# A hybrid decoder layer on one core: the matmul order of the attention written out, its steps turned round, projections in small portions

## The chip, the core and the metric

One core of a Trainium2 chip runs the whole program. Its engines are TensorE (PE in the rows; PEld is its weight load), VectorE (DVE), ScalarE (ACT), GpSimd (POOL) and SyncE (SP), which issues most of the DMAs. The metric is the device time of one execution in microseconds (us); less is better.

## The reference

The program computes one decoder layer over 1024 tokens of width 1024 in float32: a mixer with two groups of heads side by side (a chunked state-space scan, "SSD", and a stick-breaking attention of 8 heads of 64), cross attention to 256 memory tokens, and an MLP with squared ReLU. The change is in the stick-breaking attention:

```python
def stick_breaking_attention(q, k, v):
    for i in range(s_len // Q_BLOCK):              # blocks of 128 queries
        ...
        logits = jnp.einsum("bhqd,bhkd->bhqk", qb, kb) * scale
        mask = s_pos < t_pos
        log_stay = jnp.where(mask, jax.nn.log_sigmoid(-logits), 0.0)
        log_beta = jax.nn.log_sigmoid(logits)
        later = lax.cumsum(log_stay, axis=3, reverse=True) - log_stay
        w = jnp.where(mask, jnp.exp(log_beta + later), 0.0)
        outs.append(jnp.einsum("bhqk,bhkd->bhqd", w, vb))
```

A query's weight on an earlier key is the sigmoid of their score times the product of one minus the sigmoids of all keys between them. So a row of weights comes from a running product along the keys.

## The kernel before, in words

**Precision.** Every float32 product is three matmuls: each operand is split into a rounded high half (ScalarE, `act`, L107) and the remainder (VectorE, `tt`, L110), and `mm3` (L208 to L210) multiplies high by high, high by low and low by high. Weights come from memory in pieces of 128 x 512 (`piece`), land in a staging tile `wst`, and are split into `whi` and `wlo`, a ring of six.

**Attention.** Heads are taken one after the other, each in four steps m = 0 to 3. A step has two blocks of 128 queries, i = 2m and 2m + 1, with rows of 128(i + 1) keys, 128 to 1024 wide.
- `stays` makes a step's rows: score matmuls into tiles `z` (two PSUM banks, tag aux), a sigmoid on ScalarE into the row `stay`, and one scan on VectorE (L752) that turns the row into running products. Rows up to 512 wide have two buffers (tag stayS), wider ones two others (stayL).
- `turned` transposes 256 keys of both blocks on TensorE into a tile `wT` (L768; two banks, tag tr), and splits it into `wTh` and `wTl`. The last 256 keys of a step, where the causal edge lies, go into `wlast`, a pair whose unused quarter is set once; the rest is split as one slice of 256 and one of 128 columns.
- `summed` multiplies the turned weights with differences of the values, `vt` and `vl`, into a tile `ops` (L792; one bank, tag m1, OB = 1), four matmuls of 256 columns a block. Two steps share a bank; when both are done ScalarE and VectorE bring it to `oT`.

While a step is turned and summed, the next step's rows are made: `behind` holds the step to be turned, `due` the block to be summed. Per head `load_qk` and `load_v` issue DMAs from GpSimd's queue, and `differ_v` makes the value differences on VectorE and ScalarE.

**Work dealt in.** The projections of later heads and of the memory (`proj_qk`, `proj_v`, `mem_kv`; tiles `qkps`, `vps`, `mkv`, three PSUM banks, tag m0) are generators. `interleave` runs them beside the attention: whichever side has done the smaller share of its total goes on, and `("need", n)` makes the attention wait in the text until n units of projections are written. The units count 8 for each of the four that are left when the attention starts (32), the heads 7; head 7 runs beside the first half of the output projection (`out_first`, tiles `o1`). A projection yields after 24 matmuls, the attention after a whole step.

**What sets the order.** The text only gives priorities. A scheduler, with its own estimate of each instruction's time, takes on every engine the ready instruction of the highest priority; `later` shifts priorities (weight pieces come early, EARLY; splits of turned blocks a little early, WP; evacuations, EV). So single projection matmuls stand wherever the scheduler expected TensorE to wait. The built order is then fixed: each engine runs its instructions in that order.

**After head 7.** The attention's buffers are given back, and there the scaled operands `yB` of the output projection's second half are made from `oT` (four for each half of the tokens, ScalarE and VectorE). The squares of `oT` are summed into `osum`; after the first tiles (`o2`) 8 small matmuls `sps` (L975) sum them over partitions, GpSimd makes the factor `ro` (L226), and VectorE adds the tiles to `h` with it.

## Time and profile before

| | |
|---|---|
| runs | 1345.69, 1348.46, 1349.19 us; median 1348.46 |
| profiled execution | 1352.11 us, of which the span is 1350.4 |
| TensorE / VectorE / ScalarE / GpSimd busy | 1302.1 / 947.5 / 701.2 / 201.2 us |
| attention, first scan to the last widest one | 251.9 to 486.3 us of the span |
| MLP, from there on | 704 to 1341 us |

Times in the rows are from the span's start. An engine's busy time in a stretch is the union of its instructions; for TensorE each matmul's end is modelled and reaches into the next, so its busy time is more than its work. "idle before" tells for how long an engine did nothing ahead of such instructions, and the name behind the arrow ended that wait.

### The profile page before, as it was taken

How to read it: one execution, taken by the hardware profiler on the slowest of the kernel's cores; microseconds unless marked ns; L12 is line 12 of the kernel's file. 1: busy time of each engine (PE TensorE's matmuls, PEld its weight loads, DVE VectorE, ACT ScalarE, POOL GpSimd, SP SyncE). 2: the span in 40 equal slices, each digit the busy share in tenths (PEclk: the TensorE clock that was granted, in tenths of full speed). 3: DMA queues.
4: the chain of work that ended last, by engine and by line, in shares of the span. 5: the costliest groups of instructions: out<-in, count | busy, mean ns of one | idle time of the engine just before them, and what ended most of it. 6: DMA issues, size and time to landing. Idle time of an engine off the chain costs nothing.

```text
span 1350.4 us, 18360 instructions
## 1 busy us (share of the span) xinstructions
PE 1302.1 (96%) x6469; PEld 1067.1 (79%) x6469; DVE 947.5 (70%) x1527; ACT 701.2 (52%) x1341; POOL 201.2 (15%) x228
## 2 busy tenths in 40 slices
PE   8999999989998999999998999999999999999997
PEld 6989887778776788887876888888887787888885
DVE  7758866587689965646579765666667866589785
ACT  7454643465557642566445545544553595444453
POOL 0000000310211011022343323322330000000000
PEclk9999999999999999999999999999999999999999
DMA  6121345852556534121034545345459843633351
GB/s 220 33 71 48 98 124 137 238 161 68 160 149 197 155 101 125 39 56 32 33 140 148 172 156 170 123 145 164 141 172 327 304 131 95 235 95 96 96 156 70
DMA packets 95852, 181.68 MB, mean 135 GB/s; under 512 B 9808, under 2 KB 14992, under 8 KB 95760
## 3 DMA queue, kind: packets, MB, share of 16 engines
q1 hardware_dynamic: 85040, 155.78, 36.2%
q0 software_dynamic: 8624, 18.88, 5.0%
q10 hardware_dynamic: 2096, 5.84, 1.3%
q8 instruction: 51, 0.84, 0.2%
q14 instruction: 41, 0.34, 0.1%
HBM read 128.00 MB, written 52.46 MB: 134 GB/s over the span
## 4 chain that ended last, share of the span: by engine, by line
PE 81%; DVE 8%; ACT 4%; DMA 3%; issue 3%; POOL 1%; SPq 0%; POOLq 0%; ACTq 0%; DVEq 0%
PE P L210 7%; PE P L208 7%; PE P L209 7%; PE pr L208 7%; PE pr L209 7%; PE pr L210 7%; DVE stay L752 2%; PE o L210 2%; PE o L208 2%; PE o L209 2%; PE qkps L208 2%; PE qkps L209 2%; PE qkps L210 2%; DMA wst<-in_wp 2%; PE ops L792 2%
## 5 line engine op out<-in xcount | busy, mean ns | idle before, releaser
L208 PE MATMUL pr<-whi 128*128 128x512 f32 x448 | 175.9, 396 | 3.4 <-ACT whi L107 3.4
L209 PE MATMUL pr<-wlo,whi 128*128 128x512 f32 x448 | 176.9, 395 | 0.1
L210 PE MATMUL pr<-whi,wlo 128*128 128x512 f32 x448 | 176.1, 393 | 0.0
L110 POOL TENSOR_TENSOR c<-c 128x512 f32<-128x512 f32 x60 | 86.6, 1455 | 201.4 <-ACT c L107 199.1
L110 DVE TENSOR_TENSOR wlo<-w1r,whi 128x512 fp32r<-128x512 f32 x92 | 80.2, 874 | 41.9 <-ACT whi L107 41.9
L107 ACT ACTIVATE whi<-w1r 128x512 fp32r<-128x512 f32 x92 | 57.8, 630 | 94.3 <-DVE w1r L110 47.3
L208 PEld LDWEIGHTS pr<-whi 128*128 128x128 f32 x448 | 83.9, 188 | 24.8 <-ACT whi L107 4.3
L210 PE MATMUL P<-T,wlo 128*128 128x512 f32 x256 | 100.9, 394 | 1.2 <-DVE wlo L110 1.2
L208 PE MATMUL P<-T,whi 128*128 128x512 f32 x256 | 100.8, 394 | 0.0
L209 PE MATMUL P<-T,whi 128*128 128x512 f32 x256 | 100.7, 394 | 0.0
L209 PEld LDWEIGHTS pr<-wlo,whi 128*128 128x128 f32 x448 | 84.2, 188 | 20.3 <-DVE wlo L110 1.1
L210 PEld LDWEIGHTS pr<-whi,wlo 128*128 128x128 f32 x448 | 84.1, 188 | 20.2
L107 ACT ACTIVATE whi<-wst 128x512 fp32r<-128x512 f32 (+1 forms) x88 | 54.6, 630 | 78.4 <-PE o L210 30.7
L107 ACT ACTIVATE c<-c 128x512 f32<-128x512 f32 x132 | 81.5, 628 | 25.8 <-DVE c L110 24.2
L752 DVE TENSOR_TENSOR_SCAN stay<-stay,dg 128x128 f32<-128x128 f32 (+3 forms) x64 | 85.3, 1346 | 3.7 <-ACT stay L107 3.3
L107 ACT ACTIVATE whi<-us 128x512 fp32r<-128x512 f32 x64 | 40.3, 630 | 79.7 <-PE pr L209 66.8
L110 DVE TENSOR_TENSOR wlo<-wst,whi 128x512 fp32r<-128x512 f32 (+1 forms) x88 | 61.8, 715 | 24.2 <-ACT whi L107 23.1
L209 PE MATMUL P<-B,whi 128*128 128x512 f32 x192 | 76.5, 398 | 0.0
L208 PE MATMUL P<-B,whi 128*128 128x512 f32 x192 | 76.3, 397 | 0.0
L210 PE MATMUL P<-B,wlo 128*128 128x512 f32 x192 | 76.1, 396 | 0.0
L110 DVE TENSOR_TENSOR wlo<-us,whi 128x512 fp32r<-128x512 f32 x64 | 44.5, 695 | 32.3 <-ACT whi L107 31.7
L110 DVE TENSOR_TENSOR wlo<-pair,whi 128x512 fp32r<-128x512 f32 x96 | 65.7, 684 | 0.0
(340 smaller groups left out, 3387.4 us busy)
## 6 DMA issues: line engine op xcount, KB each, us to landing
ud<-c SPq DMA_DIRECT2D x112, 256.0 KB, 3.4
wst<-in_wp SPq DMA_DIRECT2D x104, 256.0 KB, 2.8
w1r<-in_wp SPq DMA_DIRECT2D x16, 1024.0 KB, 6.5
us<-ud SPq DMA_DIRECT2D x64, 256.0 KB, 2.7
pair<-in_wp SPq DMA_DIRECT2D x16, 1024.0 KB, 8.2
kk<-kd POOLq DMA_DIRECT2D x32, 256.0 KB, 5.9
p<-ud SPq DMA_DIRECT2D x24, 256.0 KB, 2.7
u<-ud SPq DMA_DIRECT2D x24, 256.0 KB, 2.7
```

The source lines that it names most:

```text
L107: nc.scalar.activation(out=out, in_=in_, func=func, **kw)
L110: (eng or nc.vector).tensor_tensor(out=out, in0=a, in1=b, op=op)
L208: nc.tensor.matmul(out=ps, lhsT=a[0], rhs=b[0], start=start, stop=False)
L209: nc.tensor.matmul(out=ps, lhsT=a[0], rhs=b[1], start=False, stop=False)
L210: nc.tensor.matmul(out=ps, lhsT=a[1], rhs=b[0], start=False, stop=stop)
L752: nc.vector.tensor_tensor_scan(out=stay[:, 0:W][:, ::-1], data0=stay[:, 0:W][:, ::-1], data1=B.dg1[:, S - W:S][:, ::-1], initial=0.0, op0= ...
L792: nc.tensor.matmul(out=ops[:, oc:oc + 256], lhsT=v, rhs=w[:, sb * 256:sb * 256 + 256], start=(s2_ == 0 and sb == 0 and j == 0), stop=(last ...
```

## The change

- `pin` ties an instruction to the last one of its kind by an order edge (`issue_after`). It is switched on for TensorE (`pinned.update({"pe"})`) while heads 0 to 6 run: there its instructions stand as the text writes them. ScalarE's and VectorE's are still placed by the scheduler. `floating` leaves weight pieces out.
- The steps of a head run as m = 0, 2, 1, 3, so that narrow and wide rows take turns. Steps 0 and 2 share a bank of `ops`, and 1 and 3.
- `stays` is cut into `scores` and `scan`, one row at a time: the attention now writes, for each turned block, the scores of a next row, the transposes, the high half (`turned`), the low half (`low`), the scan, then a portion of projections, then `summed` of the block before. The order of low half and scan varies with the step.
- Projections yield after 3 matmuls of 512 columns or 6 of 256 (0.2 units), and the attention after each block, by a table `share` that sums to 1 a head. No projection is written until heads have passed the share that was done ahead (6 of 32 units).
- The last block's used three quarters lie side by side and are split in one piece of 384 columns. `wlast` has two pairs in place of one, `wTh` and `wTl` two buffers in place of three.

```diff
+    pinned, last_ = set(), {}
+    def pin(kind, f):
+        if kind not in pinned:
+            return f()
+        if kind in last_:
+            with tc.issue_after(last_[kind]):
+                ins = f()
+        else:
+            ins = f()
+        last_[kind] = ins.ins
+        return ins
...
+    def matmul(**kw):
+        return pin("pe", lambda: nc.tensor.matmul(**kw))
...
-        nc.tensor.matmul(out=ps, lhsT=a[0], rhs=b[0], start=start, stop=False)
-        nc.tensor.matmul(out=ps, lhsT=a[0], rhs=b[1], start=False, stop=False)
-        nc.tensor.matmul(out=ps, lhsT=a[1], rhs=b[0], start=False, stop=stop)
+        matmul(out=ps, lhsT=a[0], rhs=b[0], start=start, stop=False)
+        matmul(out=ps, lhsT=a[0], rhs=b[1], start=False, stop=False)
+        matmul(out=ps, lhsT=a[1], rhs=b[0], start=False, stop=stop)
...
     def proj_v(ch, p, ps_fn):
         ws = pieces(f"v{ch}", 0, 4)
         for t in range(NT):
-            ps = tok_proj(ws, t, 256, 256, "vps", ps_fn)
+            ps = ps_fn("vps")
+            for k in range(KB):
+                mm3(ps[:, :256], (xh[k][:, t * P:(t + 1) * P], xl[k][:, t * P:(t + 1) * P]), wsl(ws, k, 0, 256),
+                    k == 0, k == KB - 1)
+                if k % 2 == 1:
+                    yield 0.2
             vt = p.tile([P, 512], F32, tag="qh", bufs=2, name="vst")[:, :256]
             with later(-EV):
                 act(vt, ps[:, :256], scale=rtok[:, t:t + 1])
             nc.sync.dma_start(out=vd[1 + t * P:1 + (t + 1) * P, 256 * ch:256 * ch + 256], in_=vt)
-            yield 1.0
+            yield 0.2
     def proj_qk(pr, p, ps_fn):
...
-                with later(GIVE):
-                  for k in range(KB):
+                for k in range(KB):
                     mm3(ps, wsl(ws, k, which * P, P), (xh[k][:, tsl], xl[k][:, tsl]), k == 0, k == KB - 1)
+                    yield 0.2
...
-                yield 2.0
+                yield 0.4
...
-            self.wlast = [[p.tile([P, 512], F32R, name=f"wlast{a}{b}") for b in range(2)] for a in range(1)]
+            self.wlast = [[p.tile([P, 512], F32R, name=f"wlast{a}{b}") for b in range(2)] for a in range(2)]
...
-            return self.p.tile([P, 512], F32R, tag=tag, bufs=3, name=tag)
+            return self.p.tile([P, 512], F32R, tag=tag, bufs=2, name=tag)
...
-        def stays(qs, ks, m):
-            out = []
-            for i in (2 * m, 2 * m + 1):
-                W = P * (i + 1)
-                stay = B.row("stay", W)
-                for off in range(0, W, 512):
-                    n = min(512, W - off)
-                    nn = max(n, 256)
-                    z = aux_ps("z")
-                    for a in range(2):
-                        nc.tensor.matmul(out=z[:, 0:nn], lhsT=qs[:, i * P:(i + 1) * P],
-                                         rhs=ks[a][off // 512][:, 0:nn], start=a == 0, stop=a == 1)
-                    act(stay[:, off:off + n], z[:, 0:n], AF.Sigmoid, scale=rq[:, i:i + 1])
-                nc.vector.tensor_tensor_scan(out=stay[:, 0:W][:, ::-1], data0=stay[:, 0:W][:, ::-1],
-                                             data1=B.dg1[:, S - W:S][:, ::-1], initial=0.0,
-                                             op0=ALU.mult, op1=ALU.max)
-                out.append(stay)
-            return out
+        def scores(qs, ks, i):
+            W = P * (i + 1)
+            stay = B.row("stay", W)
+            for off in range(0, W, 512):
+                n = min(512, W - off)
+                nn = max(n, 256)
+                z = aux_ps("z")
+                for a in range(2):
+                    matmul(out=z[:, 0:nn], lhsT=qs[:, i * P:(i + 1) * P],
+                           rhs=ks[a][off // 512][:, 0:nn], start=a == 0, stop=a == 1)
+                act(stay[:, off:off + n], z[:, 0:n], AF.Sigmoid, scale=rq[:, i:i + 1])
+            return stay
+        def scan(stay, i):
+            W = P * (i + 1)
+            pin("dve", lambda: nc.vector.tensor_tensor_scan(
+                out=stay[:, 0:W][:, ::-1], data0=stay[:, 0:W][:, ::-1], data1=B.dg1[:, S - W:S][:, ::-1],
+                initial=0.0, op0=ALU.mult, op1=ALU.max))
...
-                    o = sb * 256 + ii * P
+                    o = (256 - sb * 256 if last else sb * 256) + ii * P
                     b = 2 * s2_ + sb
-                    nc.tensor.transpose(out=t4[:, o:o + P], in_=wb[ii][:, b * P:(b + 1) * P], identity=ident)
+                    transpose(out=t4[:, o:o + P], in_=wb[ii][:, b * P:(b + 1) * P], identity=ident)
+            if last:
+                wh, wl = B.wlast[nl_[0] % len(B.wlast)]
+                nl_[0] += 1
+                sl = slice(P, 512)
+            else:
+                wh, wl = B.wT("wTh"), B.wT("wTl")
+                sl = slice(0, 512)
             with later(-WP):
-                if last:
-                    wh, wl = B.wlast[nl_[0] % len(B.wlast)]
-                    nl_[0] += 1
-                    for sl in (slice(0, 256), slice(384, 512)):
-                        split(wh[:, sl], wl[:, sl], t4[:, sl])
-                else:
-                    wh, wl = B.wT("wTh"), B.wT("wTl")
-                    split(wh, wl, t4)
-            return wh, wl
+                act(wh[:, sl], t4[:, sl])
+            def low():
+                with later(-WP):
+                    tt(wl[:, sl], t4[:, sl], wh[:, sl].bitcast(F32), ALU.subtract)
+            return (wh, wl), low
...
+            hh, last, oc = h % 2, s2_ == m, 256 * (m // 2)
+            if (h, m % 2) not in opss:
+                opss[h, m % 2] = psum("m1", OB, "ops")
+            ops = opss[h, m % 2]
...
-        steps = [(h, m) for h in range(8) for m in range(4)]
+                    matmul(out=ops[:, oc:oc + 256], lhsT=v, rhs=w[:, o:o + 256],
+                           start=(s2_ == 0 and sb == 0 and j == 0), stop=(last and sb == 1 and j == 1))
+            if last and m // 2 == 1:
+                od = oT[64 * hh:64 * hh + 64, h // 2, :].rearrange("p (a b c) -> p a b c", a=2, b=2)[:, :, m % 2, :]
+                act(od, ops[64:128, :].rearrange("p (a c) -> p a c", a=2), scale=-1.0)
+                tt(od, od, ops[0:64, :].rearrange("p (a c) -> p a c", a=2), ALU.subtract)
+        steps = [(h, m) for h in range(8) for m in (0, 2, 1, 3)]
+        share = {0: (0.27,), 2: (0.06, 0.06, 0.07), 1: (0.12, 0.28), 3: (0.03, 0.03, 0.04, 0.04)}
         behind, due, qk = None, None, None
         for h, m in steps + [(8, 0)]:
-            rows = None
+            rows, todo = [], []
             if h < 8:
-                if m == 0:
-                    if h == 0:
-                        yield ("need", need(0))
-                        load_v(0)
-                    qk = load_qk(h)
-                rows = stays(*qk, m)
-                if (h, m) == (0, 0):
-                    differ_v(0, False)
-            if behind is not None:
+                todo = [2 * m, 2 * m + 1]
+            if behind is None:
+                yield ("need", need(0))
+                load_v(0)
+                qk = load_qk(0)
+                for i in todo:
+                    rows.append(scores(*qk, i))
+                    scan(rows[-1], i)
+                differ_v(0, False)
+            else:
                 h_, m_, wb = behind
-                if m_ == 0 and due is not None:
-                    summed(*due)
-                    due = None
                 for s2_ in range(m_ + 1):
-                    ws = turned(m_, s2_, wb)
+                    i = todo.pop(0) if todo and (m_ < 3 or s2_ > 0) else None
+                    if i is not None:
+                        rows.append(scores(*qk, i))
+                    ws, low = turned(m_, s2_, wb)
+                    if m_ == 0 and todo:
+                        rows.append(scores(*qk, todo[0]))
+                        scan(rows[0], i)
+                        low()
+                        scan(rows[1], todo.pop())
+                    else:
+                        low()
+                        if i is not None:
+                            scan(rows[-1], i)
+                    if m_ == 1 and s2_ == 1 and h_ < 7:
+                        qk = load_qk(h_ + 1)
+                    if m_ == 0 and due is not None:
+                        summed(*due)
+                        due = None
+                    if m_ == 3 and s2_ == 2 and h_ < 7:
+                        differ_v(h_ + 1)
+                    yield share[m_][s2_]
                     if due is not None:
                         summed(*due)
                     due = (h_, m_, s2_, ws)
                 if h == 8 or (h_, m_) == (pause, 3):
                     summed(*due)
                     due = None
-                if h_ < 7 and m_ == 1:
+                if h_ < 7 and m_ == 2:
                     yield ("need", need(h_ + 1))
                     load_v(h_ + 1)
-                elif h_ < 7 and m_ == 2:
-                    differ_v(h_ + 1)
-                yield (3.0 + 4.0 * m_) / 36.0
                 if (h_, m_) == (pause, 3):
                     yield "pause"
             behind = (h, m, rows)
...
+    pinned.update({"pe"})
     interleave(chain(*[filler(*f, qk_ps) for f in late]), till_pause(heads_), 8.0 * len(late), float(NHA))
+    pinned.clear()
```

TensorE's order at the turn of a head's step. The names: `z` scores, `wT` transposes, `ops` value matmuls, `vps` and `qkps` projections. Before, in head 1, where rows of 768 and 384 keys are scored:

```order
L749 MATMUL z<-kk,qs 128x512 x2
L749 MATMUL z<-kk,qs 128x256 x2
L792 MATMUL ops<-wlast_2253,vt 128x256
L792 MATMUL ops<-wlast_2252,vl 128x256
L768 MATMUL wT<-ident,stay 128x128
L208 MATMUL vps<-whi,xh_106 128x256
L209 MATMUL vps<-wlo,xh_106 128x256
L749 MATMUL z<-kk,qs 128x256 x2
L749 MATMUL z<-kk,qs 128x384 x2
L792 MATMUL ops<-wlast_2253,vl 128x256
L768 MATMUL wT<-ident,stay 128x128
L749 MATMUL z<-kk,qs 128x512 x2
```

After, at the same place of head 1:

```order
L137 MATMUL z<-kk,qs 128x384 x2
L140 MATMUL wT<-ident,stay 128x128 x4
L137 MATMUL qkps<-xh_106,whi 128x512
L137 MATMUL qkps<-xl_114,whi 128x512
L137 MATMUL qkps<-xh_106,wlo 128x512
L137 MATMUL ops<-wlast_2252,vt 128x256
L137 MATMUL ops<-wlast_2253,vt 128x256
L137 MATMUL ops<-wlast_2252,vl 128x256
L137 MATMUL ops<-wlast_2253,vl 128x256
L137 MATMUL z<-kk,qs 128x512 x2
L140 MATMUL wT<-ident,stay 128x128 x4
L137 MATMUL qkps<-xh_107,whi 128x512
```

Before, scores of both steps stand close together and transposes, value matmuls and projections are mixed one by one; now each portion follows the last as a block: scores, four transposes, three projection matmuls, four value matmuls of the block before.

TensorE's order where the attention ends, in head 7, which is not pinned. `o1` is the output projection's first half, `o2` its second, on `yB`. Before:

```order
L792 MATMUL ops_4969<-wTl_5129,vt_4495 128x256
L792 MATMUL ops_4969<-wTh_5128,vt_4495 128x256
L792 MATMUL ops_4969<-wTl_5129,vt_4495 128x256
L792 MATMUL ops_4969<-wlast00_2252,vt_4495 128x256
L792 MATMUL ops_4969<-wlast01_2253,vt_4495 128x256
L792 MATMUL ops_4969<-wlast00_2252,vl_4496 128x256
L210 MATMUL o1_5154<-whi_5071,yS0_4712 128x512
L792 MATMUL ops_4969<-wlast01_2253,vl_4496 128x256
L208 MATMUL o1_5154<-whi_5077,yS0_4712 128x512
L209 MATMUL o1_5154<-wlo_5078,yS0_4712 128x512
L210 MATMUL o1_5154<-whi_5077,yS0_4712 128x512
L208 MATMUL o1_5170<-whi_5059,yS0_4712 128x512
```

After:

```order
L140 MATMUL wT_5182<-ident_69,stay_4937 128x128
L140 MATMUL wT_5182<-ident_69,stay_5018 128x128 x2
L137 MATMUL ops_5110<-wTh_5160,vt_4601 128x256
L137 MATMUL ops_5110<-wTl_5161,vt_4601 128x256
L137 MATMUL ops_5110<-wTh_5160,vt_4601 128x256
L137 MATMUL ops_5110<-wTl_5161,vt_4601 128x256
L137 MATMUL ops_5110<-wlast10_2254,vt_4601 128x256
L137 MATMUL ops_5110<-wlast11_2255,vt_4601 128x256
L137 MATMUL ops_5110<-wlast10_2254,vl_4602 128x256
L137 MATMUL ops_5110<-wlast11_2255,vl_4602 128x256
L137 MATMUL o2_5274<-whi_5252,yB0_5213 128x512
L137 MATMUL o2_5274<-wlo_5253,yB0_5213 128x512
```

Before, the last value matmuls have `o1` among and behind them (75 of 192 `o1` matmuls come after the last one); now `o2` follows the last value matmul, and all 192 stand ahead of it.

## Rows read from the trace of the kernel before

**Rows 1.** Stretches of heads 0 to 7: length, engines' busy (instructions), clock, DMA share, GB/s

```profile
251.90:272.10 20.20, 18.20 (x104) 14.27 (x102) 17.56 (x25) 13.09 (x28) 2.65 (x5) 1.00 0.69 213
272.10:296.50 24.40, 19.91 (x137) 17.03 (x137) 21.41 (x33) 16.37 (x37) 4.50 (x7) 1.00 0.57 146
296.50:319.30 22.80, 20.54 (x145) 18.22 (x145) 19.70 (x29) 14.82 (x32) 4.52 (x7) 1.00 0.39 109
319.30:351.70 32.40, 31.69 (x219) 28.44 (x220) 21.51 (x34) 17.88 (x40) 4.50 (x7) 1.00 0.35 97
351.70:383.70 32.00, 27.86 (x151) 22.79 (x150) 22.33 (x34) 15.98 (x34) 4.22 (x6) 0.95 0.46 136
383.70:414.10 30.40, 27.53 (x155) 21.96 (x155) 27.05 (x43) 21.25 (x46) 5.58 (x9) 1.00 0.62 184
414.10:447.40 33.30, 29.23 (x158) 22.29 (x158) 30.51 (x50) 23.62 (x50) 2.92 (x4) 1.00 0.66 199
447.40:486.30 38.90, 37.57 (x208) 31.84 (x209) 32.39 (x49) 22.54 (x44) 1.27 (x8) 0.96 0.37 116
```

**Rows 2.** TensorE in order of time: start us, us, line, out<-in, count

```profile
496.09 0.60 PE L768 MATMUL wT<-ident,stay 128*128 128x128 f32 x4
...
520.14 0.39 PE L208 MATMUL o<-whi,yB 128*128 128x512 f32 x1
...
525.70 1.84 PE L975 MATMUL sps<-ones,osum 128*128 128x1 f32 x16
```

**Rows 3.** Who waited for whom, TensorE, 251 to 503 us: total us, times, longest

```profile
PE wT L768 <- DVE stay L752: 11.1, 18, 1.4
PE ops L792 <- ACT wTh L107: 4.9, 4, 2.4
```

**Rows 4.** The page's groups, the scan: busy us, mean ns | idle before

```profile
L752 DVE TENSOR_TENSOR_SCAN stay<-stay,dg 128x128 f32<-128x128 f32 (+3 forms) x64 | 85.3, 1346 | 3.7 <-ACT stay L107 3.3
```

**Rows 5.** VectorE's groups by shape, 251 to 503 us

```profile
L110 DVE TENSOR_TENSOR wTl<-wT,wTh 128x512 fp32r<-128x512 f32 x48 | 32.3, 682 | 12.8 <-ACT wTh L107 12.6
...
L752 DVE TENSOR_TENSOR_SCAN stay<-stay,dg 128x1024 f32<-128x1024 f32 x8 | 18.2, 2281 | 0.1
...
L110 DVE TENSOR_TENSOR wlast<-wT,wlast 128x256 fp32r<-128x256 f32 x32 | 13.2, 413 | 1.3 <-ACT wlast L107 1.2
...
L110 DVE TENSOR_TENSOR wlast<-wT,wlast 128x128 fp32r<-128x128 f32 x32 | 8.8, 276 | 2.4 <-ACT wlast L107 2.4
```

**Rows 6.** ScalarE and VectorE in order of time, the last block of head 7

```profile
500.85 0.39 ACT L107 ACTIVATE wlast<-wT 128x256 fp32r<-128x256 f32 x1 [0.21 <-PE wT L768]
501.28 0.41 DVE L110 TENSOR_TENSOR wlast<-wT,wlast 128x256 fp32r<-128x256 f32 x1
...
501.73 0.28 ACT L107 ACTIVATE wlast<-wT 128x128 fp32r<-128x128 f32 x1 [0.49 <-DVE wlast L110]
...
502.04 0.29 DVE L110 TENSOR_TENSOR wlast<-wT,wlast 128x128 fp32r<-128x128 f32 x1 [0.34 <-ACT wlast L107]
```

**Rows 7.** ScalarE's groups by shape, 251 to 503 us

```profile
L107 ACT ACTIVATE stay<-z,rq 128x512 f32<-128x512 f32 x48 | 32.7, 691 | 3.5 <-PE z L749 3.0
L107 ACT ACTIVATE wTh<-wT 128x512 fp32r<-128x512 f32 x48 | 28.2, 596 | 22.8 <-PE wT L768 22.2
```

**Rows 8.** The chain of waits, 251 to 503 us: start, us, what

```profile
346.49 6.20 DMA v<-vd
```

**Rows 9.** One stretch, columns as in rows 1

```profile
351.00:356.00 5.00, 2.61 (x19) 2.28 (x19) 4.03 (x8) 3.20 (x8) 0.71 (x1) 0.95 1.10 347
```

**Rows 10.** ScalarE, GpSimd, VectorE in order of time, after head 7

```profile
503.48 1.34 ACT L107 ACTIVATE yB<-oT,colt 128x512 fp32r<-128x512 f32 x2
...
504.73 3.78 ACT L107 ACTIVATE yB<-oT,colt 128x512 fp32r<-128x512 f32 x6
...
527.83 1.68 POOL L226 TENSOR_TENSOR ro<-rv,nhalf 128x8 f32<-128x8 f32 x1 [15.08 <-DVE rv L114]
...
529.54 2.07 DVE L117 SCALAR_TENSOR_TENSOR h<-o,ro,h 128x512 f32<-128x512 f32 x3 [1.80 <-POOL ro L226]
```

## What is expected, and why

> **What bounds the kernel now.** I read the table of stretches first, cut at the end of each head's widest scan. It gives each head of the attention its own row [rows 1]: heads 0 to 6 fill 251.9 to 447.4 us, 195.5 us in all, and head 7 ends its widest scan at 486.3. The reader is to see that no engine is full there. VectorE is busy 17.6, 21.4, 19.7, 21.5, 22.3, 27.1 and 30.5 us of the seven heads, 160 of 195.5 (82%). TensorE's column looks fuller than it is, because the duration of a matmul overlaps the next one: two tiles of the output projection, 24 matmuls of 512 columns, pass between 520.14 and 525.70 [rows 2], so one costs 0.232 us and not the 0.39 that stands beside it; four transposes take 0.60 with the last one's latency in it, some 0.11 each. Counting by these prices (a matmul of 256 columns at half, of 384 at three quarters) a head's attention needs 24 score matmuls = 4.4 us, 36 transposes = 3.9 and 40 value matmuls = 4.7: 13.0 us of TensorE. The projections worked in during heads 0 to 6 (by the order, 202 of 512 columns and 192 of 256) are 69 us. That is 160 of 195.5 for TensorE too. So 35 us are lost in which neither engine has its limit, and the table of waits says to whom: transposes for the scan, value matmuls for ScalarE's half of the split [rows 3]. A scan takes 10.7 us a head in eight pieces, the widest 2.28 [rows 4, 5].
>
> **The change, part by part.**
>
> Work removed. The last block of each step was split as 256 and 128 columns, and is now one piece of 384. On VectorE 0.413 + 0.276 goes and something between the 0.413 of 256 columns and the 0.682 of 512 comes [rows 5]; on the line through the three it is 0.55, a gain of 0.14 each. 28 of them are 3.9 us of VectorE in heads 0 to 6. On ScalarE 0.39 + 0.28 goes [rows 6], about 0.49 comes. Neither engine is full, so this pays mainly as latency: the four halves run in a row, 500.85, 501.28, 501.73, 502.04, ready at 502.33 [rows 6], 1.48 us; in one piece 0.49 + 0.55 + 0.04 = 1.08.
>
> The Trainium skill, "Perfetto Trace Analysis", section Optimizing Scalar/DVE Operations, says that where these engines are not saturated but cause bubbles on others, breaking instructions up lets work end sooner. By that rule the merge costs: the first half was ready 0.84 us after its start, the whole now after 1.08, 0.24 later, up to 6.7 us over 28 blocks. The trace disagrees, since the second ScalarE half starts only after VectorE's first (they share a tile). I go by the rows.
>
> Order of the steps. Rows up to 512 wide have two buffers and wider ones two others. In the old order 0, 1, 2, 3 step 1 scores into the buffers that step 0's transposes still read, and step 3 into those of step 2. In 0, 2, 1, 3 each step scores into the other pair, so the scans of the next step run while this one is turned. This takes away the reason of most of the 11.1 us [rows 3]. What is late next I get by following a head by hand with these durations (first pieces 0.05 us apart). PE and VectorE by step: step 0 5.7 and 4.4 us, step 2 5.8 and 4.1, step 1 8.5 and 6.2, step 3 5.6 and 5.9, 25.6 and 20.6 with 12.8 us of projections dealt in by the share table. TensorE then waits some 1.2 us in step 0 (two score tiles of the second row need the two PSUM banks of the first, behind two 0.69 activations [rows 7]), 0.2 for the widest scan, 0.5 behind the differences of the next head's values, which hold VectorE 2.2 us (two operations of 512 and two of 256 columns at the prices of [rows 5]). That is 27.6; with 0.15 of restart at each of five waits 28.3 us a head. Two buffers for a turned block in place of three cost nothing in it: its low half is done before TensorE turns the next but one (0.1 a block if not).
>
> Fixed order. The scheduler used to drop single projection matmuls into any gap; now a fixed portion stands at each place, and a wait at the head of the queue holds the projections behind it. The share at which projections run also moves: six of 32 units are done before head 0, so by the pacing rule none comes until 1.31 heads are through. There VectorE sets the pace: by hand 19.6 us for head 0 to the end of its widest scan and 24 for head 1, 43.6 against 44.6. Heads 2 to 4 are 3 x 28.3 = 85 against 87.2. That head 4 took 32.0 before came also from its values' load, 6.2 us, around which TensorE was busy 2.6 of 5 us [rows 8, 9]; now the last value projection stands a whole step 1 and half a step 3 ahead of the differences that need it, some 11 us, which covers that load. Heads 5 and 6 carry the memory's weight splits on VectorE, 27.1 and 30.5 busy [rows 1]; the same work less 1.1, at 95% of VectorE, is 59.5 against 63.7. Sum: 188 against 195.5, **-7 us**. Bounds: at the larger of the two engines' needs heads 0 and 1 are 38, 2 to 4 77, 5 and 6 56.5; that 171.5 at 95% gives 180 (-15). Every head from 2 on at 32, as heads 3 and 4 were, gives 43.6 + 160 = 204 (+8). The value I take is the hand-followed head's.
>
> Head 7, not fixed, has the first half of the output projection as cover, 192 matmuls. Before, 117 of them stood ahead of its last value matmul and 75 behind; now all 192 are ahead. With more work to put in the gaps I take -2 of the 38.9 [rows 1] (0 to -4).
>
> The end of attention is the edit's price. Those 75 matmuls, 17.4 us, covered what follows: the last head's evacuation, then the scaled operands yB, which live in memory that the attention gives back, the sum of squares and the factor ro. Before, yB was begun at 503.48 [rows 10] and first used at 520.14 [rows 2]. Now nothing is left to cover it. After the last value matmul: 0.2 latency, the evacuation 0.6 and a weight's split 0.6 that stands between on ScalarE (both priced as 512 columns [rows 7]), then the first of eight yB at 0.63 each [rows 10]: TensorE starts at about 2.1 us, waits a little for VectorE's halves, and ends four tiles at 12.8. PSUM has four banks for them, and none is freed without ro. The sums take 1.84 us with their latency [rows 2], ro begins 0.29 later and takes 1.68, the first add 0.69 [rows 10]: TensorE goes on at 17.3, where its own work was 13.0. So 4.3 us are new, and about 0.7 ahead of them, where the last block's split now stands bare. Less what was lost there before (0.5): **+4.5** (+2 if the splits slip ahead, +7 if the load of weights is late too).
>
> The earlier SSD stretch changes only in where value projections stand among the chunk work; TensorE is full there either way: 0 (+-1.5).
>
> Sum: -7 - 2 + 4.5 + 0 = -4.5 us. The profiled execution took 1352.1 (span 1350.4 and 1.7 around it), 3.7 over the median of the runs, 1348.46; I take the difference off the median: **1344**.
>
> **Rivals.**
> First, the fixed order keeps VectorE fed throughout and heads 2 to 6 come near their larger engine's need: 180 in place of 188. For it: VectorE idles 18% over heads 0 to 6, and TensorE's waits there are for VectorE and ScalarE, not for data [rows 3]. Against: heads 5 and 6 leave little, 89 and 92% [rows 1]. -15.5 - 2 + 4.5 = -13: 1335.5.
>
> Second, slower: waits at the head of TensorE's queue. Each portion's value matmuls wait for a split whose VectorE place was chosen apart; if a weight split of 0.68 or the differences slip in ahead, TensorE stands and the projections behind it cannot fill in, as they did. From 4 us of such waits a head on, five heads lose more than the rest brings. For it: value matmuls already waited 4.9 us in four waits, the longest 2.4 [rows 3]. Against: the portions' sums leave VectorE slack in three of four steps. +8 - 1 + 4.5 = +11.5: 1360.
>
> Third, the clock. In the rows of heads 4 and 7 the granted clock is 0.95 and 0.96 [rows 1], so a part of each ran at 1.2 in place of 2.4 GHz, worth 5% of 32.0 and 4% of 38.9, 1.6 us each, and ahead of the first fall TensorE had stood half idle [rows 9]. The new idle places are heads 0 and 1 and the 2.7 us behind the sums. Two more falls there, 1.6 each: 1347, no change. The Trainium skill, "TensorE: Matmul & The Clock Gate", section HAM oscillation, says that idle gaps between bursts send the clock back to half; the two rows agree, and no run here shows yet that these places trip it.
>
> **Numbers.** Forecast 0.42, first rival 0.22, second 0.22, third 0.10; 0.04 that the order changes nothing visible, 1348. A difference of 0.3%, 4.05 us, is what this measurement can tell. The forecast lies at that edge: of its 0.42 I give 0.23 to faster, 0.16 to the same, 0.03 to slower. Faster 0.23 + 0.21 = 0.44; same 0.16 + 0.08 + 0.04 + 0.02 = 0.30; slower the rest, 0.26. Range 1331 to 1360: from the first rival's value less 4 (heads 5 and 6 at their need) to the second's; the forecast's own is 1338 to 1350.
>
> **What would show it.** Right: waits of transposes for the scan under 5 us; heads 2 to 4 near 28 us; in heads 0 and 1 no projections; the first matmul on yB within 3 us of the last value matmul, then a gap of some 2.5 us behind the sums' matmuls. Wrong: if heads 2 to 4 stay at 30 or more with value matmuls waiting for VectorE, the second rival; if no gap follows the sums, the last term fails and the time is near 1339; if the clock falls anew in heads 0 and 1, the third.

## The result and the profile after

The changed kernel takes 1372.93 us (median of 4 runs, 1370.66 to 1375.41) against 1348.45: a ratio of 1.0183 with the interval 1.0167 to 1.0199, slower by 24 us where 1344 was forecast with 1331 to 1360 around it. Its profiled execution has a span of 1371.1 us, 20.7 more than before. The profiled execution of the kernel before lay 3.7 us above its median and the one after at its own, so 20.7 of the 24 us can be followed in the traces.

First the table of stretches, cut as in [rows 1]: heads 0 to 7, then two stretches of the output projection's second half.

```profile
253.00:273.00 20.00, 14.18 (x62) 10.78 (x62) 15.05 (x16) 10.40 (x19) 2.65 (x5) 0.76 0.48 120
273.00:301.30 28.30, 25.22 (x141) 21.80 (x141) 21.00 (x27) 16.14 (x30) 4.51 (x7) 0.88 0.26 77
301.30:333.40 32.10, 28.29 (x205) 26.10 (x204) 21.30 (x28) 17.08 (x36) 4.52 (x7) 0.95 0.47 138
333.40:362.30 28.90, 27.91 (x200) 25.59 (x198) 22.79 (x33) 19.76 (x40) 5.25 (x8) 1.00 0.42 119
362.30:388.30 26.00, 25.61 (x148) 21.80 (x149) 20.09 (x26) 14.10 (x27) 3.46 (x5) 1.00 0.52 150
388.30:418.30 30.00, 29.18 (x168) 24.39 (x166) 28.65 (x44) 21.41 (x43) 5.55 (x9) 1.00 0.75 208
418.30:457.10 38.80, 31.29 (x148) 25.96 (x148) 29.45 (x43) 23.03 (x44) 2.91 (x4) 0.82 0.53 162
457.10:510.80 53.70, 50.18 (x273) 41.26 (x272) 38.85 (x54) 25.24 (x46) 3.35 (x13) 1.00 0.43 129
532.40:539.20 6.80, 6.17 (x15) 4.82 (x16) 6.13 (x10) 6.80 (x11) 1.14 (x2) 0.50 1.14 305
549.50:556.30 6.80, 4.51 (x11) 3.57 (x12) 2.73 (x4) 0.00 (x0) 1.36 (x1) 0.50 0.00 0
```

The column to read is the granted clock, behind the five engines. Before it was 1.00 in six of the eight heads; now it is 0.76, 0.88, 0.95 and 0.82 in heads 0, 1, 2 and 6, and 0.50 (1.2 GHz) in the last two rows. VectorE's column has hardly moved (158.3 us in heads 0 to 6 against 160.1), so it isn't the bound. Head 7 is long because the matmuls `o1` that used to follow it now stand in it.

The waits of TensorE in heads 0 to 6, columns as in [rows 3]:

```profile
PE ops L137 <- ACT wTh L130: 6.3, 2, 3.4
PE wT L140 <- DVE stay L795: 5.3, 5, 1.8
PE z L137 <- ACT stay L130: 5.0, 10, 2.8
PE mkv L137 <- DVE ql L147: 3.7, 1, 3.7
...
PE ops L137 <- DVE oT L133: 2.0, 1, 2.0
```

Before, in the same heads:

```profile
PE wT L768 <- DVE stay L752: 9.6, 16, 1.4
```

The wait for the scan has nearly halved, from 9.6 to 5.3 us (from 11.1 to 6.0 with head 7, the stretch of [rows 3]). Five single waits of 2 to 3.7 us at the head of TensorE's queue stand out: two for ScalarE's half (2.9 and 3.4), one of the ten for a score bank (2.8), one for `ql` (3.7) and one for `oT` (2.0). The longest before was 2.4. At the end of the attention, TensorE and GpSimd's factor in order of time, which answer to [rows 2] and [rows 10]:

```profile
533.03 0.79 PE L137 MATMUL o<-whi,yB 128*128 128x512 f32 x1 [2.08 <-ACT yB L130]
...
547.05 1.84 PE L1041 MATMUL sps<-ones,osum 128*128 128x1 f32 x16
...
551.79 0.77 PE L137 MATMUL o<-whi,yB 128*128 128x512 f32 x1 [2.90 <-DVE h L147]
...
549.19 1.67 POOL L256 TENSOR_TENSOR ro<-rv,nhalf 128x8 f32<-128x8 f32 x1 [15.64 <-DVE rv L144]
```

From inside each of the two waits, 2.08 and 2.90 us, on runs one of the two stretches at half clock. They hold 15 and 11 matmuls in 6.8 us, where 29 would fit at 0.232 (the first 0.6 us of the one and 2.3 us of the other still belong to the wait).

Where the 20.7 us arose, from the times at which the same instructions start or end in both traces:

| from, to | before | after | difference |
|---|---|---|---|
| start, to the first score matmul | 251.1 | 249.6 | -1.5 |
| to the end of head 6's widest scan | 196.3 | 207.5 | +11.2 |
| to the last value matmul | 55.4 | 73.9 | +18.5, of which 17.4 are the 75 `o1` moved ahead: +1.1 |
| to the last matmul of the output projection | 68.9 | 61.7 | -7.2, and 17.4 moved away: +10.2 |
| to the end | 778.6 | 778.4 | -0.2 |

For heads 0 to 6 I split TensorE's loss: for each matmul, the time to the next one's start less its price at the full clock (0.231, 0.117 and 0.10 us for 512 columns, 256 and a transpose). In a stretch at half clock up to one such price goes to the clock; of the rest, what is over 0.15 us in one piece is a wait. Before: waits 27.0, clock 1.4, the rest 11.2. After: waits 31.0, clock 12.8, the rest 7.5. Less was waited in small pieces, a little more in large ones, and 11.4 us went to the clock.

### The profile page after: what moved, and what is told of

It is laid out like the page before. It is cut to its first block, busy times and chain, and to the rows that moved or that the text cites. A ratio compares the mean times of both kernels' runs of the same rounds, so it can differ in the third digit from the quotient of the medians.

```text
span 1371.1 us, 18282 instructions
## 1 busy us (share of the span) xinstructions
PE 1313.1 (96%) x6469; PEld 1081.1 (79%) x6469; DVE 947.8 (69%) x1495; ACT 700.7 (51%) x1309; POOL 199.1 (15%) x230
## 4 chain that ended last, share of the span: by engine, by line
PE 82%; DVE 8%; DMA 4%; ACT 3%; issue 3%; POOL 1%; SPq 0%; POOLq 0%; ACTq 0%; DVEq 0%
PE P L137 22%; PE pr L137 22%; PE o L137 7%; PE qkps L137 4%; PE xsps L137 3%; PE xqps L137 3%; PE vps L137 3%; PE xops L137 3%; DMA wst<-in_wp 3%; DVE stay L795 2%; PE z1ps L137 2%; PE ops L137 2%; PE zdps L137 2%; PE z L137 2%; PE wT L140 1%
## 5 line engine op out<-in xcount | busy, mean ns | idle before, releaser
L137 PE MATMUL P<-T,whi 128*128 128x512 f32 x512 | 160.3, 394 | 0.3 <-DVE T L133 0.3
L137 PE MATMUL P<-B,whi 128*128 128x512 f32 x384 | 121.3, 397 | 0.0
L137 PEld LDWEIGHTS P<-T,whi 128*128 128x128 f32 x512 | 96.2, 188 | 22.9 <-DVE T L133 0.8
L137 PEld LDWEIGHTS P<-B,whi 128*128 128x128 f32 x384 | 72.5, 189 | 16.9
L130 ACT ACTIVATE stay<-z,rq 128x512 f32<-128x512 f32 (+2 forms) x96 | 53.2, 579 | 30.3 <-PE z L137 23.7
```

The costliest lines, as they stand in the source:

```text
L130: return pin("act", lambda: nc.scalar.activation(out=out, in_=in_, func=func, **kw))
L137: return pin("pe", lambda: nc.tensor.matmul(**kw))
```

## The experiments

**The pin alone.**

```diff
-    pinned.update({"pe"})
```

> The changed kernel with TensorE's order left to the scheduler (the pin is never switched on); steps, portions and splits stay as changed. Theory (the fixed order keeps projections out of heads 0 and 1 and out of the waits, so that the granted clock falls): heads 0 to 6 come back from 204 us to 190 to 196, the falls of the clock in heads 0 to 2 and 6 are mostly gone (half clock in heads 0 to 6 under 10 us, against 34), and the time is 1358 to 1364, still above the kernel before by the bare end of the attention, about 10 us. Rival (the order of the steps and the small portions cost the time, the pin does not): 1368 to 1374.

Measured 1346.99 us (12 runs), ratio to the kernel before 0.9981 (0.9968 to 0.9995). The theory's direction holds and its size was too small: without the pin heads 0 to 6 take 178.3 us from scan to scan (181.5 from the first score matmul), and no stretch in them is at half clock. The profiled execution was the quickest of the twelve, 1342.79, so its stretches flatter this kernel by some 4 us; the differences of medians are the safer measure. (The kernel before ran again beside the experiments, with medians of 1348.67 to 1349.88 us; a microsecond between two runs says nothing.) Heads 0, 1, 2, 3, 4, 5 and 6:

```profile
253.90:271.40 17.50, 15.68 (x87) 11.31 (x87) 16.62 (x20) 12.19 (x24) 2.65 (x5) 1.00 0.69 178
271.40:292.10 20.70, 18.48 (x128) 15.97 (x128) 20.59 (x28) 15.96 (x33) 4.51 (x7) 1.00 0.63 158
292.10:315.70 23.60, 23.54 (x181) 22.24 (x182) 18.82 (x25) 13.99 (x28) 4.51 (x7) 1.00 0.38 104
315.70:344.40 28.70, 27.97 (x200) 25.68 (x198) 22.82 (x34) 19.83 (x40) 5.26 (x8) 1.00 0.43 123
344.40:370.00 25.60, 25.53 (x148) 21.85 (x149) 20.03 (x27) 14.02 (x27) 3.46 (x5) 1.00 0.54 155
370.00:400.40 30.40, 28.66 (x166) 24.27 (x165) 28.70 (x44) 21.96 (x44) 5.55 (x9) 1.00 0.75 210
400.40:432.20 31.80, 28.05 (x158) 22.62 (x157) 29.08 (x44) 22.90 (x46) 2.93 (x4) 1.00 0.63 194
```

Heads 3 to 5 take the same with and without the pin (28.9, 26.0, 30.0 against 28.7, 25.6, 30.4). All of the pin's cost stands in heads 0 to 2 and 6. In head 0 TensorE has 87 instructions here against 62, 22 of them `qkps`: the scheduler has pulled projections forward that the text deals out only later. With the pin the first projection stands at 285.95 us. TensorE's loss in heads 0 to 6, split as above, is here 15 us of waits, nothing by the clock and 9 of the rest: the pin costs some 16 us of waits and 13 by the clock, less 2 of the rest.

**The end of the attention.**

```diff
-    interleave(out_first(), heads_, 17.6, 8.0 - NHA)
+    interleave(out_first(), heads_, 10.0, 8.0 - NHA)
```

> The changed kernel with the first half of the output projection held back in head 7 (its share counted against 10.0 in place of 17.6), so that 81 of its 192 matmuls stand behind the last value matmul, as 75 did before the change. Theory (10 of the 20 us are the bare end: 2.1 and 2.9 us of waits and two falls of the clock of 6.8 us at half): the waits of the first matmul on yB and behind the sums are under 0.5 us, neither fall is there, and the time is 1361 to 1365. Rival (the loss at the end belongs to the late start of the operands and only moves): 1368 to 1373.

Measured 1363.15 us, ratio 1.0096 (1.0082 to 1.0110): the theory. TensorE waits for nothing from 505 to 582 us, and the clock is 1.00 there. From the end of head 6's widest scan to the last matmul of the output projection it is 125.8 us, against 135.6 after the change and 124.4 before. The bare end is worth 10 us.

**Extra work at the end.** Matmuls without a use, in the waits themselves, while the waits stay.

```diff
     interleave(out_first(), heads_, 17.6, 8.0 - NHA)
+    idle = qk_ps("warmps")
+    for _ in range(12):
+        matmul(out=idle, lhsT=yS[0][:, 0, 0, 0:P], rhs=yS[0][:, 0, 0, :], start=True, stop=True)
...
+                idle = aux_ps("warmps")
+                for _ in range(3):
+                    matmul(out=idle, lhsT=osum[:, 0:P], rhs=osum[:, 0:512], start=True, stop=True)
                 ro = rstd_of(cpl, sps[:, :NT], NT, 512, "ro")
```

> The changed kernel with extra matmuls whose results nobody uses in the two waits at the end of the attention: 12 of 512 columns around and behind the last value matmuls (9 behind them), and 3 of 512 columns in full float32 behind the sums of squares. Theory of the clock (of the 10 us lost there, 5 are waits, which stay, and 4 to 5 are the two stretches of 6.8 us at half clock behind them): no fall between 525 and 560 us, and the time falls by 2 to 5, to 1368 to 1371, though work is added. Rival (the stretches at half clock go with the waits and cost little): 1373 to 1376.

Measured 1366.39 us, ratio 1.0133 (1.0118 to 1.0147): the theory, and by the medians more than it, 6.5 us less with work added. TensorE there, and the windows of the two stretches after the change (the second one here begins behind its wait):

```profile
529.99 2.21 PE L137 MATMUL warmps<-yS 128*128 128x512 f32 x9
532.11 0.51 PE L137 MATMUL o<-whi,yB 128*128 128x512 f32 x1
...
545.23 2.82 PE L137 MATMUL warmps<-osum 128*128 128x512 f32 x6
548.27 0.47 PE L137 MATMUL o<-whi,yB 128*128 128x512 f32 x1 [0.21 <-DVE h L147]
```

```profile
532.40:539.20 6.80, 6.80 (x30) 5.19 (x30) 6.13 (x9) 6.80 (x10) 0.34 (x1) 1.00 1.20 337
549.50:556.30 6.80, 6.80 (x31) 5.54 (x30) 2.10 (x3) 0.00 (x0) 0.00 (x0) 1.00 0.00 0
```

The matmuls on yB still begin where their operands are ready, 2.0 us behind the last value matmul, and then run at the full clock: 30 and 31 in 6.8 us. From the last value matmul to the last of the output projection it is 56.9 us, 4.8 less than after the change. This much is shown as the extra work's own; the rest of the 6.5 lies elsewhere in the profile, where nothing was added. So of the 10 us, half is waiting and half is the clock behind the waits. The Trainium skill, "TensorE: Matmul & The Clock Gate", section HAM oscillation, says that idle gaps between bursts send the clock to half for the next burst. The rows agree in kind: 0.50 from the waits of 2.08 and 2.90 us on, 1.00 where they were filled. The gaps that the section tells of are longer, and end with data from memory.

**Extra work in heads 0 and 1.** In the fixed order, where no projection stands:

```diff
...
+            if not isinstance(v, tuple) and done < 1.31:
+                n = int(v * 4.57 / 0.4 + 0.5)
+                if n:
+                    ps = qk_ps("warmps")
+                    for _ in range(3 * n):
+                        matmul(out=ps, lhsT=xh[0][:, 0:P], rhs=xh[1][:, 0:512], start=True, stop=True)
...
```

> The changed kernel with extra work: some 40 matmuls of 512 columns, whose results nobody uses (about 9 us of TensorE at full clock), are written in the fixed order at the places of the projections' portions while heads 0 and 1 run, where no projection stands. Theory of the clock (heads 0 to 2 lose 9 us to half clock): with the extra work the half clock in the first three heads drops from 20 us to under 8, the widest scan of head 1 ends no later than now (301.3), and the time is 1364 to 1371. Rival (TensorE's waits as such are the loss; added work only adds): head 1 ends 3 to 9 us later and the time is 1374 to 1380.

Measured 1369.36 us, ratio 1.0142 (1.0129 to 1.0156): with 42 matmuls more, 9.7 us of TensorE, its median is 3.6 us lower. Half clock in the first three heads fell from 20.5 us to 10.2, not under 8 as expected; the first row's fall, behind the start, stayed. Heads 0, 1, 2 and 6:

```profile
252.90:273.40 20.50, 19.30 (x92) 15.67 (x92) 14.59 (x16) 10.07 (x19) 2.65 (x5) 0.83 0.40 93
273.40:299.70 26.30, 24.72 (x152) 21.23 (x153) 21.36 (x29) 16.01 (x30) 4.51 (x7) 1.00 0.34 101
299.70:332.20 32.50, 28.55 (x205) 26.36 (x205) 21.43 (x29) 16.98 (x36) 4.51 (x7) 0.95 0.47 134
...
417.10:452.60 35.50, 27.41 (x149) 22.61 (x148) 28.99 (x44) 22.46 (x44) 2.93 (x4) 0.95 0.57 177
```

Heads 0 to 2 take 79.3 us in place of 80.4: the added work paid for itself, with 1.1 us over. The larger part of what the profile gained, 3.3 us, stands in head 6, where nothing was added. That head's half clock varies from profile to profile, and it took 36.1 us with the held half and 38.0 with the extra work at the end, the text of its steps being the same.

**Projections from head 0 on, order fixed.**

```diff
-            if live_a and (not live_b or da / total_a <= db / total_b):
+            if live_a and (not live_b or (da - base) / (total_a - base) <= db / total_b):
```

with the six units done ahead as `base`.

> The changed kernel with the projections dealt out evenly from head 0 on (the share that is done ahead is taken off both sides of the comparison), order fixed as changed. Theory of the clock: heads 0 and 1 keep the full clock, the falls at 252 to 290 us are gone or shorter, and the time is 1363 to 1368. Rival (the cover is only taken from later heads, which lose as much): heads 2 to 6 are longer by what heads 0 and 1 gain, 1370 to 1375.

Measured 1357.29 us, ratio 1.0047 (1.0033 to 1.0061), 15.6 us below the changed kernel and beyond the theory: heads 0 to 2 take 73.7 us (22.6, 25.9, 25.2) in place of 80.4, with one fall of 3.4 us left in head 0, and head 6 takes 30.3 in place of 38.8. Head 3 is longer (32.2): a wait of 3.9 us for ScalarE's half behind a late weight piece and 6.8 us at half clock stand there now. In all seven, waits are 24.4 us and the clock's part 5.0. The rival fell: heads 2 to 6 take 143.1 us with the new pacing from 301.6 on, where the changed kernel has 155.8. Head 6's two waits, told of below, are gone with it.

**The pin from the end of head 1 on.**

```diff
...
+            done += 0.0 if isinstance(v, tuple) else v
+            if done > 1.9:
+                pinned.add("pe")
...
```

> The changed kernel with TensorE's order fixed from the end of head 1 on in place of from head 0, so that the scheduler may pull projections forward into heads 0 and 1. Theory (the fixed order costs in two ways: 10 us in heads 0 and 1, where the text has no projections and the clock falls, and some 13 us in heads 2 to 6, where waits for splits and evacuations stand at the head of the queue): head 1 ends at 291 to 294 us in place of 301, heads 2 to 6 keep 152 to 157 us, and the time is 1362 to 1366. Rival (all of the loss starts in heads 0 and 1): heads 2 to 6 take 140 to 145 us and the time is 1350 to 1355.

Measured 1355.32 us (10 runs, 1351.26 to 1362.58), ratio 1.0045 (1.0030 to 1.0060), at the edge of the rival's span: heads 0 and 1 as without the pin, heads 2 to 6 150.1 us, between the two, where the pinned kernel has 155.8 and the free one 140.1. The profiled execution was the quickest of the ten, 4.1 us under the median, as that of the free kernel was. Heads 0, 1, 2 and 6:

```profile
252.90:270.30 17.40, 15.67 (x87) 11.29 (x87) 16.51 (x20) 12.18 (x24) 2.65 (x5) 1.00 0.67 181
270.30:291.10 20.80, 18.02 (x122) 15.26 (x122) 20.70 (x29) 15.51 (x32) 4.50 (x7) 1.00 0.62 158
291.10:318.50 27.40, 26.26 (x188) 24.48 (x189) 18.96 (x24) 14.66 (x29) 4.51 (x7) 0.94 0.32 93
...
403.40:441.20 37.80, 28.78 (x149) 23.87 (x148) 29.16 (x44) 22.58 (x44) 2.93 (x4) 0.91 0.57 166
```

So some 10 us of the loss start in heads 0 and 1 (head 1 ends at 291.1 in place of 301.3), and head 6 is a second place of its own. The chain of waits of the changed kernel shows what happens there (start, duration, what):

```profile
414.80 7.33 DMA wst<-in_wp
...
422.23 0.64 ACT whi L130
422.87 0.02 issue
422.89 0.69 DVE wlo L133
423.59 0.61 DVE wTl L133
424.20 0.04 issue
424.24 0.80 PE ops L137 x2
```

A weight piece is late. ScalarE's and VectorE's order was not pinned, and the scheduler put its split ahead of that of a turned block; TensorE stood 3.4 us before that block's value matmuls, with projections behind them. Later a projection `mkv` waited 3.7 us for its bank, which VectorE emptied (`ql`) only after the differences and two scans. The clock fell behind both. The first of the two waits is not the pin's alone: without it the same value matmul waits 2.3 us at this place, and 3.05 us in the version without the pin and with the held half, where 6.8 us at half clock follow. The wait for the bank is in pinned kernels only.

**The order of the steps, and the portions, each taken back in the kernel without the pin.**

```diff
...
-        steps = [(h, m) for h in range(8) for m in (0, 2, 1, 3)]
+        steps = [(h, m) for h in range(8) for m in range(4)]
...
```

> The changed kernel without the pin and with the steps of a head in the old order 0, 1, 2, 3 (with the banks of the value tiles, the loads of the next head's queries, keys and values at the places that go with it). Theory (of the 15 us by which heads 0 to 6 are shorter without the pin than before the change, the order of the steps brings most, since each step's rows are scored into the other pair of buffers): waits of transposes for the scan are back at 8 to 12 us, heads 0 to 6 take 190 to 196 us in place of 181, and the time is 1355 to 1362. Rival (the small portions or the writing order inside a step bring it): 1344 to 1350.

Measured 1352.63 us (12 runs), ratio 1.0023 (1.0010 to 1.0036), a little under the theory's span; heads 0 to 6 take 188.4 us. The wait that the order was to remove is back:

```profile
PE wT L140 <- DVE stay L795: 10.2, 19, 1.0
```

Without the pin and with the new order it is 4.7. By the medians the order is worth 5.6 us; the 188.4 stand against 178.3 in the quickest execution of the kernel without the pin, and 181.0 in the version with the held half. The portions:

```diff
-                if k % 2 == 1:
-                    yield 0.2
...
-            yield 0.2
+            yield 1.0
```

(and the same for queries and keys, 2.0 a tile; the memory's projections keep their small portions.)

> The changed kernel without the pin and with the projections written 24 matmuls at a time, as before the change. Theory (the scheduler moves single matmuls into the gaps whatever portions the text has): heads 0 to 6 within 3 us of the run without the pin, 1344 to 1350. Rival (the portions bring the 15 us): heads 0 to 6 take 190 us or more, 1354 to 1362.

Measured 1353.60 us (12 runs), ratio 1.0032 (1.0020 to 1.0043). The theory fell: heads 0 to 6 take 190.3 us, as the rival had it, and the time is 6.6 us over the kernel with small portions, just below the rival's span. Value matmuls wait 6.1 us in two waits for ScalarE's half (2.3 with small portions), and the clock falls twice. Why the scheduler leaves those waits with large portions was not settled.

**The last block in two pieces, without the pin.**

```diff
-                act(wh[:, sl], t4[:, sl])
+                act(wh[:, sls[0]], t4[:, sls[0]])
...
+                    for x, sl in enumerate(sls):
+                        if x:
+                            act(wh[:, sl], t4[:, sl])
+                        tt(wl[:, sl], t4[:, sl], wh[:, sl].bitcast(F32), ALU.subtract)
```

> The changed kernel without the pin and with the last block of a step split in two pieces, 256 and 128 columns, each ScalarE then VectorE, as before the change. Theory by the rows of before (two pieces are 1.48 us in a row, one is 1.08, and VectorE has 0.14 us more a block): the same or up to 6 us longer, 1347 to 1353. Rival by the rule that smaller pieces let the waiting engine start sooner: 1341 to 1346.

Measured 1349.88 us (12 runs), ratio 1.0008 (0.9994 to 1.0021), 2.9 us over one piece, with intervals that just touch: within the theory's span, no gain as the rival had it, and too little to call a loss. VectorE's rows, two pieces here:

```profile
L133 DVE TENSOR_TENSOR wlast<-wT,wlast 128x256 fp32r<-128x256 f32 x32 | 13.2, 413 | 2.2 <-ACT wlast L130 2.2
L133 DVE TENSOR_TENSOR wlast<-wT,wlast 128x128 fp32r<-128x128 f32 x32 | 8.9, 279 | 3.2 <-ACT wlast L130 3.1
```

and one in the changed kernel:

```profile
L133 DVE TENSOR_TENSOR wlast<-wT,wlast 128x384 fp32r<-128x384 f32 x32 | 17.5, 548 | 2.1 <-ACT wlast L130 2.0
```

**A version that beats both kernels.** No pin, and `o1` held back (the edits of the first two runs):

> TensorE's order left to the scheduler and the first half of the output projection held back in head 7, together. Theory (the pin costs heads 0 to 6, the bare end costs its own time, and the two add up): heads 0 to 6 end at 432 us as without the pin, from there to the last matmul of the output projection 126 us as with the held half in place of 132, so 1339 to 1343. Rival (the scheduler had already used what the holding gives): 1345 to 1349.

Measured 1337.87 us (5 runs, 1337.41 to 1338.65), ratio 0.9912 (0.9898 to 0.9926): 11 us under the kernel before, a little under the theory's span. The two gains add up: 25.9 and 9.8 us by the medians one at a time, 35.1 together. From the end of head 6's widest scan to the last matmul of the output projection it is 123.7 us, with no wait of TensorE from 480 to 560 us. With projections from head 0 on as well:

> TensorE's order left to the scheduler, the output projection's first half held back in head 7, and the projections dealt out evenly from head 0 on. Theory (the scheduler pulls projections forward by itself, and heads 0 to 2 were already short): within 3 us of the run without the even dealing, 1335 to 1341. Rival (covering heads 0 and 1 fully leaves later heads bare): 1342 to 1347.

Measured 1342.47 us, ratio 0.9951 (0.9938 to 0.9963): worse than without, and the rival's time. Heads 0 to 6 take 187.4 us in place of 181.0, of which head 1 alone is 9.1 longer and head 6 6.6 shorter: two value matmuls wait 2.8 and 3.9 us for ScalarE behind weights that took 7.1 and 6.6 us to land, and 10 us are at half clock. What helped the fixed order here hurt the free one.

## Why the prediction was wrong

- **Work removed.** Right: 384 columns take 0.548 us, forecast 0.55, and 0.49 on ScalarE. In the last block of head 7 the two halves take 1.09 us from start to end, forecast 1.08. The Trainium skill, "Perfetto Trace Analysis", section Optimizing Scalar/DVE Operations, says that smaller pieces may let work end sooner. Two pieces that alternate between the engines brought no gain here: 1349.88 us against 1346.99.
- **Order of the steps.** Right: the wait for the scan went from 11.1 [rows 3] to 6.0 us in the whole attention, a little over the 5 that was named as its sign. Heads 2 to 4 came to 32.1, 28.9 and 26.0, 87.0 against 85, but the 28.3 a head followed by hand holds only in the mean; head 2 has a wait of 2.9 us.
- **Fixed order.** This step failed: that a fixed order costs no more than the waits followed by hand. Heads 0 to 6 are 204.1 us against 188, and the run without the pin shows that the pin alone costs 26 us by the medians, some 16 of waits and 13 by the clock in the traces. Of the 16 us over the forecast 4.7 lie in heads 0 and 1, 2.0 in 2 to 4 and 9.3 in 5 and 6. For heads 0 and 1 I wrote that "VectorE sets the pace" and took 43.6 us; they are 48.3, though VectorE is busy only 36.1. That no projections stand there was seen; that TensorE, left alone, would wait and then run the scores, transposes and value matmuls at 1.2 GHz was left to the third rival, at two falls of 1.6 us. At the start alone it stood 2.79 us before the second step's scores, for a bank that a sigmoid on ScalarE was to free; ahead of that sigmoid ScalarE emptied a projection and loaded a table for 1.28 us:

```profile
252.99 1.94 PE L137 MATMUL z<-kk,qs 128*128 128x512 f32 x4 [2.79 <-ACT stay L130]
...
251.28 1.28 ACT L130 ACT_TABLE_LOAD   x1
```

  Four matmuls of 512 columns then take 1.94 us. The kernel before has eight `qkps` matmuls at this place. The measure that I missed is what the scheduler did before: 24 `qkps` and 5 `vps` stand in head 0, where the pinned order has none, and 41 `vps` in head 1, where it has 24 `qkps` and 18 `vps`, the first at 285.95 us. Those of head 0 and a part of those of head 1 were pulled forward past the pacing of the text, and the pin forbade it. Heads 5 and 6 were put at 59.5 and are 68.8, by the two waits in head 6 and the clock. Sum for heads 0 to 6: -7 forecast, +11.2 measured from the first score matmul. Without the pin they are -14.8 in the quickest execution, near the first rival's -15.5, and -12.5 in the version with the held half.
- **Head 7.** -2 forecast, +1.1 measured: it loses 3.3 us to five small waits in its first 18, before the `o1` matmuls come.
- **The end of the attention.** The mechanism was right, the size was not: this term was mis-sized too. First matmul on yB 2.1 us forecast and 2.08 measured; gap behind the sums 2.7 and 2.90. The term of +4.5 measured +10.2, and the run with extra work shows 4.8 of the missing part to be the clock after each gap. A slip of the sum is in it as well: 48 matmuls at 0.232 from 2.1 on end at 13.2, not 12.8.
- **SSD stretch.** 0 +- 1.5 forecast, -1.5 measured; the first score matmul stands at 249.4 to 251.2 in the profiles of the six pinned kernels, so this is scatter.
- **The rivals.** The second (waits at the head of the queue, 1360) and the third (the clock) were priced as if each came alone. Both came, at the same places: at the start, in head 6 and at the end of the attention the clock fell behind a wait.

Head 6's two waits are in the profiles of all five pinned kernels with the old pacing (2.5 to 4.4 and 3.7 to 4.3 us), and not in the one with even pacing, which has the first one in head 3. The first is in the kernels without the pin too (2.3 and 3.05 us): it comes from ScalarE's order, in which a late weight piece stands ahead. Whether fixing ScalarE's order as well would take it away was not tried.

## What to carry to other kernels

Fixing an engine's order forbids more than it orders: look first for what the scheduler had pulled forward past the text's own pacing, and put it into the text at those places before pinning (the even pacing won back 15.6 of the pin's 25.9 us). Price a new long wait of TensorE at up to twice its length: at the end of the attention 5 us of waits cost 10, by the 1.2 GHz behind them. Not every wait costs so much; without the pin one of 2.3 us in head 6 was followed by no fall. When work is moved ahead of a point, ask what it covered behind it.

## What the runs showed of the hardware

Matmuls whose results nobody uses, put into waits, made the kernel shorter although they add work: 15 at the end of the attention took 4.8 us off the stretch where they stand, and 42 in heads 0 and 1, 9.7 us of work, left heads 0 to 2 shorter by 1.1. Three matmuls of 512 columns in full float32 (six records in the row) took 2.82 us, 0.94 each against 0.23 for the split operands. Single weight pieces took 6.6 to 7.33 us to land, where the median of their kind in the changed kernel is 2.8, and ScalarE, with the work on such a piece next in its order, held up value matmuls of TensorE for 2.8 to 3.9 us.
